# Five buffer counts and lead times of a planned schedule, and one sum moved from VectorE to a transfer, in a one-core attention trunk

## The chip, the core and the metric

One NeuronCore of one Trainium2 chip runs the whole program. TensorE (PE) multiplies matrices, VectorE (DVE) and ScalarE (ACT) work element by element, GpSimd (POOL) and SyncE (SP) here do little but issue transfers (DMA). The metric is device time in microseconds (us). The kernel before took 1747.45, 1742.09 and 1746.84 us in three runs, median 1746.84.

## The reference

The input is a residual stream of 256 tokens by 4096 channels, all in float32. Depth is one, so one layer runs, the attention layer:

```python
proj = rms_norm(x, norm_attn) @ w_in_attn        # 256x4096 @ 4096x16384 -> q | k | v | gate
o = stick_breaking_attention(q, k, v)            # 32 heads of 128
h = x + (o * silu(gate)) @ w_out_attn            # 256x4096 @ 4096x4096
return rms_norm(h, final_norm)
```

In the attention each weight is `sigmoid(z_ts) * prod_{s<j<t} (1 - sigmoid(z_tj))` for `s < t`, computed in log space with a suffix sum. The two projections are nearly all of the work: 320 MiB of float32 weights are read once.

## The kernel before

**Units.** The input projection is cut into 16 units. A unit makes 256 columns of each of q, k, v and gate, which is two heads. The output projection is cut into 4 more units of 1024 columns. A unit runs over the 4096 rows of its weights in 8 steps of 512 rows. One step needs 2 MB of weights, loaded as four *raw quarter tiles* of 128x1024 float32 (512 KB each, two 256 KB transfers from SP's queue). `raw{q}_{t}{k}` is the quarter of step q (counted over the whole program, 8 per unit) with column half t and row half k.

**Parts and products.** A matmul of float32 precision is made of three fast ones in the type fp32r: the operands are split into a high and a low half, and high*high, high*low and low*high are added up in PSUM. So for each *part* (a 128x1024 slice of weights) ScalarE casts the raw tile to fp32r (`wh{n}`, the high half), VectorE subtracts that from the raw tile (`wl{n}`, the low half), and then PE runs two to four *products*, each of three 128x128 by 128x512 matmuls. The names say it: `acc<-wh,sh` multiplies high by high, `acc<-wl,sh` is the matmul that first needs the low half (sh, sl: the halves of the activations in the input projection; oh, ol in the output projection).

**Seven instead of eight multiplications.** Some steps use a 2x2 scheme with seven block products in place of eight (Strassen and Winograd). Such a *seven step* has 7 parts and 14 products, and needs sums of raw tiles first: one is made by an accumulating transfer while weights are loaded (called T3 in the code; `raw<-in_w_in_dram` from POOL's queue), the other three by VectorE (`raw<-raw,raw`), or, in steps 1 and 3 of the input projection, the last of the three by an accumulating transfer between two tiles in the core's own memory (T4; `raw<-raw` from POOL's queue). An *eight step* has 4 parts and 16 products and no sums; a *mixed step* does half of its rows each way (6 parts, 15 products, three half-size sums). A unit of the input projection after the first has steps 1, 3, 4, 6 seven, 0, 2, 5 mixed and 7 eight: 117 products. In the output projection 1, 3, 6 are seven, 0, 2, 5 mixed, 4 and 7 eight: 119 products. The first unit of each projection is plain: 128 products.

**Evictions.** The products of a unit are added up in seven PSUM banks (`acc{u}_1` to `acc{u}_7`). When a unit ends, `combine` (L805) takes the banks out with VectorE and ScalarE into `qk_sb` and `gv_sb` (in the output projection into `h`). A bank that the next unit writes again has to be out before PE may start in it. Each input unit's two heads are computed while the next unit's products run, with small matmuls between the products (`ten`, L399).

**The planner.** Nothing of the order on the engines is written by hand. While the program is built, the class `Plan` plays it as a queue of events with costs per instruction; each engine takes, among the work that is ready, that with the smallest *key* (a due time in PE's time), and the order so found is the order in the program. Buffers are counted in *rings* (L413): a raw tile is taken before its load and given back when the last reader is done, a place for a low half is taken before the subtraction and given back when PE has finished the part. The same counts are the numbers of real buffers. On the chip every engine then works through its list strictly in order, and waits on semaphores.

The constants that matter here: `RAW_BUFS` (L46) raw quarter tiles; `PAIRS` (L47) high halves; `LOWS` (L47) low halves; `KEPT` (L48), the number of the program's last parts whose products are put in order of the PSUM bank (banks 4 and 5 first, then 2, then 3; L357), so that the last banks fill one after the other; `T3_LEAD` (L57), the time that the planner adds to the planned landing of an accumulating transfer before it lets its readers start; `FOURTH_IN`, `FOURTH_OUT` (L58), the seven steps whose last sum goes by transfer; `TEN_WAIT` (L62), the time that the planner lets pass before it offers a head's matmuls to PE; `EVICT` (L71), by how much the key of a unit's evictions on VectorE lies before the start of the next unit:

```python
key = place_of[u + 1, 0] - EVICT                                  # combine
fourth = not mixed and parts[a]["s"] in (FOURTH_IN if parts[a]["u"] < OUT0 else FOURTH_OUT)
```

`last_h` (L1208) and `finish` (L1291) end the program: token half 1 of the last 1024 columns is complete with banks 4 and 5, its sum of squares gives `factor1`, and the eight 128x512 tiles of that half are scaled and written; half 0 follows with banks 2 and 3 and `factor0`.

Of the kernel before, what the change touches and what calls it, by code (L numbers as in the profile page):

```python
# [42 lines left out]

SEVEN_IN, MIX_IN = (1, 3, 4, 6), (0, 2, 5)
SEVEN_AFTER, MIX_AFTER = (1, 3, 6), (0, 2, 5)
RAW_BUFS = 8  # L46
PAIRS, LOWS = 6, 6  # L47
KEPT = 6  # L48
LAST_STEPS = (2, 6, 5, 1, 0, 3, 7, 4)
LATE_FROM, LATE_BEHIND = 4, 1  # L50

# [2 lines left out]
HEADS_LATER = 12  # L54
AHEAD, SUMS_AHEAD = 1.0, 3.0
PIPE = 1
T3_LEAD = 1500  # L57
FOURTH_IN, FOURTH_OUT = (1, 3), ()  # L58
FOURTH_AHEAD = 6.0
RAW_LEAD = 0  # L60
EARLY = 2.5
TEN_WAIT = 1200  # L62
QK_LEAD = 2000
CAST_AHEAD = 3.0
BLOCKS_LATER = 2
# [2 lines left out]
FORM_LEAD = 0  # L68
STATS = 2, 10
AWAY, PLACE_H = (0, 1, 2), (0, 1, 0, 1, 0, 2)  # L70
EVICT = 0  # L71


PLAIN = {"C11": 1, "C21": 4, "C12": 7, "C22": 6}
# [60 lines left out]
def tensor_ns(n):  # L135
    return 0.4167 * n + 13.4 if n > 128 else 109.0
# [137 lines left out]
def kernel(  # L274
# [76 lines left out]
    n_parts = len(parts)  # L351
    kept = range(n_parts - KEPT, n_parts)
    begun = len(PLAIN_PARTS) * NS
    order = [(n, k) for n in range(begun) for k in range(len(parts[n]["prods"]))]
    order.sort(key=lambda e: (parts[e[0]]["s"], parts[e[0]]["prods"][e[1]][2]))
    order += [(n, k) for n in range(begun, n_parts - KEPT) for k in range(len(parts[n]["prods"]))]
    for banks in ((4, 5), (2,), (3,)):  # L357
# [41 lines left out]
    def ten(emit, *n):  # L399
        return nc.work("tensor", 90 + sum(tensor_ns(m) for m in n), emit, nc.here - 1e4, wait=TEN_WAIT)  # L400

# [10 lines left out]
    for name, places in (  # L412
        ("raw", RAW_BUFS), ("w", PAIRS), ("low", LOWS), ("gh", 3), ("one", 1), ("two", 1),  # L413
        ("qkh", 1), ("qkl", 1), ("f", 1), ("att", 1), ("heads", 1),
# [12 lines left out]
    def load():  # L427
# [8 lines left out]
        for _, q, t, k in sorted(tiles):  # L436
            if 1 < q < NS:
                yield nc.until(("used", 0, max(HALF * q - LOAD_AHEAD, 0)))
            yield nc.take("raw")
            raw[q, t, k] = wp.tile([P, HG, HALF, CW], F32, tag="raw", name=f"raw{q}_{t}{k}", bufs=RAW_BUFS)  # L440
            if seven[q] and (t, k) == (1, 0):
# [54 lines left out]
    def sums(q):  # L496
# [16 lines left out]

        yield nc.until(("T3", q), lead=T3_LEAD)
        yield nc.until(("lows", a))
# [9 lines left out]
        def moved_third():  # L525
# [5 lines left out]
            )  # L531
            yield nc.until(("T4", q), lead=T3_LEAD)
            nc.tell(("sums", g[0]))
# [271 lines left out]
    def combine(u, one, two, what):  # L805

        bank = ev[u]
        key = place_of[u + 1, 0] - EVICT

# [309 lines left out]
    def fetch():  # L1119

        yield nc.until("loaded", ("h", NJ - 3, 1))
        for c in AWAY:
            yield nc.take("raw")
            both = wp.tile([P, HG, HALF, CW], F32, tag="raw", name=f"back{c}", bufs=RAW_BUFS)
            for t in range(NT):
# [318 lines left out]
```

## Time and profile before

| | |
|---|---|
| three runs | 1747.45, 1742.09, 1746.84 us |
| the profiled execution | 1742.72 us, span of the core 1741.0 us, mean granted TensorE clock 0.996 |
| busy in the span | PE 1713.9, VectorE 1630.2, ScalarE 1227.0, POOL 209.1 us |
| DMA | 434.84 MB, mean 250 GB/s |

In the profile a row of a group gives the line, engine and operation, then out<-in by the program's names without numbers, the count, busy time and mean; "idle before" is the time that the engine stood still just before such an instruction, and the arrow names what ended it. Nearly all instructions carry line L158, that of the helper which records them, so the tiles' names tell them apart. A row of a timeline gives the start, the length and, in square brackets, the idle time before. PEld is the weight-load side of PE. A matmul's row lasts 0.39 us because neighbours overlap; the pitch from start to start is what counts.

### The profile page before, as it was taken

What the parts mean: (1) busy time and instruction counts of PE and PEld (TensorE: products, weight loads), DVE (VectorE), ACT (ScalarE), POOL (GpSimd) and SP (SyncE); (2) the same over time, 40 slices, a digit from 0 to 9 for tenths busy, and PEclk for the clock granted to TensorE, in tenths of its full rate; (3) what the DMA queues carried; (4) which work ended last, traced back from release to release, by engine and by line L of the source; (5) the groups of instructions that cost most, each with busy time, mean ns of one, the idle gap of its engine ahead of it and who ended that gap; (6) DMA issues with size and microseconds to landing.
All of it is one profiled execution on the core that took longest, in us unless ns stands there. A gap on an engine that the chain in (4) does not pass through costs nothing.

```text
span 1741.0 us, 23954 instructions
## 1 busy us (share of the span) xinstructions
PE 1713.9 (98%) x7690; PEld 1407.4 (81%) x7690; DVE 1630.2 (94%) x1872; ACT 1227.0 (70%) x1599; POOL 209.1 (12%) x224
## 2 busy tenths in 40 slices
PE   9999999999999999999999999999999999999997
PEld 6888888888888888888787878787888778888885
DVE  7889999999999999999999999999999987899997
ACT  7876777676777676767686767676767665666664
POOL 0010111011101011111111111111111022011100
PEclk9999999999999999999999999999999999999998
DMA  9998989888989898988888988889898778798886
GB/s 302 316 251 242 254 243 241 239 252 254 243 253 248 249 239 254 238 252 236 250 242 246 237 250 232 247 235 260 232 258 236 254 251 241 232 290 243 261 255 230
DMA packets 240543, 434.84 MB, mean 250 GB/s; under 512 B 25472, under 2 KB 45440, under 8 KB 240416
## 3 DMA queue, kind: packets, MB, share of 16 engines
q1 hardware_dynamic: 197616, 354.24, 62.0%
q0 software_dynamic: 41504, 77.22, 24.4%
q10 hardware_dynamic: 1296, 1.85, 0.3%
q8 instruction: 60, 0.98, 0.2%
q14 instruction: 67, 0.55, 0.1%
HBM read 407.52 MB, written 9.96 MB: 240 GB/s over the span
## 4 chain that ended last, share of the span: by engine, by line
PE 65%; DVE 13%; DMA 11%; issue 5%; ACT 4%; SPq 1%; POOL 0%; ACTq 0%; DVEq 0%; POOLq 0%
PE acc L158 62%; DMA raw<-in_w_in_dram 8%; DVE wl L158 8%; ACT wh L158 3%; DVE raw L158 3%; PE z L158 2%; DMA xres<-in_x_dram 1%; PE o L158 1%; SPq L158 1%; DMA p<-spill 1%; PE tr L158 1%; DMA raw<-in_w_out_dram 1%; ACT f L158 0%; DVE qk_sb L158 0%; DVE h L158 0%
## 5 line engine op out<-in xcount | busy, mean ns | idle before, releaser
L158 ACT CAST wh<-raw 128x1024 fp32r<-128x1024 f32 (+1 forms) x959 | 941.9, 1021 | 393.1 <-DMA raw<-in_w_in_dram 201.2
L158 DVE TENSOR_TENSOR wl<-raw,wh 128x1024 fp32r<-128x1024 f32 (+1 forms) x959 | 1100.8, 1184 | 60.3 <-ACT wh L158 57.0
L158 PE MATMUL acc<-wh,sh 128*128 128x512 f32 x1883 | 751.6, 399 | 4.3 <-DVE qk_sb L158 2.5
L158 PE MATMUL acc<-wl,sh 128*128 128x512 f32 x1883 | 735.9, 391 | 6.7 <-DVE wl L158 6.0
L158 PE MATMUL acc<-wh,sl 128*128 128x512 f32 x1883 | 735.6, 391 | 0.0
L158 PEld LDWEIGHTS acc<-wl,sh 128*128 128x128 f32 x1883 | 354.5, 188 | 85.2 <-DVE wl L158 15.7
L158 PEld LDWEIGHTS acc<-wh,sh 128*128 128x128 f32 x1883 | 354.2, 188 | 77.0 <-DVE qk_sb L158 5.8
L158 PEld LDWEIGHTS acc<-wh,sl 128*128 128x128 f32 x1883 | 353.8, 188 | 75.5 <-DVE sl L158 0.2
L158 DVE TENSOR_TENSOR raw<-raw,raw 128x1024 f32<-128x1024 f32 (+1 forms) x339 | 326.2, 964 | 2.0
L158 POOL DMA_DIRECT2D raw<-in_w_in_dram x105 | 127.9, 1218 | 931.6 <-DMA raw<-in_w_in_dram 522.9
L158 PE MATMUL acc<-wl,oh 128*128 128x512 f32 x485 | 189.5, 391 | 2.2 <-DVE wl L158 2.1
L158 PE MATMUL acc<-wh,oh 128*128 128x512 f32 x485 | 189.9, 391 | 0.0
L158 PE MATMUL acc<-wh,ol 128*128 128x512 f32 x485 | 188.8, 389 | 0.0
L158 PEld LDWEIGHTS acc<-wl,oh 128*128 128x128 f32 x485 | 91.1, 188 | 23.2 <-DVE wl L158 4.8
L158 PEld LDWEIGHTS acc<-wh,ol 128*128 128x128 f32 x485 | 91.1, 188 | 18.8
L158 PEld LDWEIGHTS acc<-wh,oh 128*128 128x128 f32 x485 | 91.1, 188 | 18.7
L158 ACT ACTIVATE f<-f 128x384 f32<-128x384 f32 x96 | 50.5, 526 | 3.0
L158 POOL DMA_DIRECT2D raw<-raw x30 | 26.5, 882 | 208.9 <-ACT f L158 86.7
L158 ACT CAST oh<-p 128x512 fp32r<-128x512 f32 (+3 forms) x41 | 19.3, 488 | 32.5 <-DVE p L158 16.6
L158 POOL DMA_DIRECT2D raw<-in_w_out_dram x18 | 21.5, 1192 | 136.2 <-DMA raw<-in_w_out_dram 105.4
L158 DVE SCALAR_TENSOR_TENSOR gv_sb<-acc,rin_v,gv_sb 128x512 f32<-128x512 f32 x45 | 33.5, 745 | 0.7
L158 POOL DMA_DIRECT2D p<-spill x41 | 22.9, 567 | 90.4 <-DVE ol L158 84.7
(88 smaller groups left out, 749.3 us busy)
## 6 DMA issues: line engine op xcount, KB each, us to landing
raw<-in_w_in_dram SPq DMA_DIRECT2D x1016, 256.0 KB, 5.0
raw<-in_w_out_dram SPq DMA_DIRECT2D x256, 256.0 KB, 5.1
raw<-in_w_in_dram POOLq DMA_DIRECT2D x60, 512.0 KB, 8.7
raw<-raw POOLq DMA_DIRECT2D x30, 512.0 KB, 6.8
raw<-in_w_in_dram POOLq DMA_DIRECT2D x45, 256.0 KB, 6.3
p<-spill POOLq DMA_DIRECT2D x41, 128.0 KB, 4.7
raw<-in_w_out_dram POOLq DMA_DIRECT2D x9, 512.0 KB, 8.8
xr<-in_x_dram SPq DMA_DIRECT2D x16, 256.0 KB, 5.5
```

Of the source, the lines that this page charges most:

```text
L158: return self.tc.keep_in_program_order(getattr(self.engine, name)(*args, **kw))
```

## The change

Six constants are different. The core gets nine raw quarter tiles (before: eight) and five places for low halves (six); both kinds take 4 KB per partition, so the sum is the same. Five parts (six) are ordered by bank at the end. The planner reckons with 2000 ns (1500) after an accumulating transfer, and with 1000 ns (1200) before a head's matmuls. In the output projection the last sum of step 1 goes by an accumulating transfer. The key of VectorE's evictions lies 3000 ns earlier.

```diff
-RAW_BUFS = 8
-PAIRS, LOWS = 6, 6
-KEPT = 6
+RAW_BUFS = 9
+PAIRS, LOWS = 6, 5
+KEPT = 5
...
-T3_LEAD = 1500
-FOURTH_IN, FOURTH_OUT = (1, 3), ()
+T3_LEAD = 2000
+FOURTH_IN, FOURTH_OUT = (1, 3), (1,)
...
-TEN_WAIT = 1200
+TEN_WAIT = 1000
...
-EVICT = 0
+EVICT = 3000
```

Through the planner the order on every engine shifts, though PE's products keep theirs up to the last unit's kept parts, and SP's loads of raw tiles keep theirs nearly everywhere. VectorE has three sums fewer (`raw137_01`, `raw145_01`, `raw155_01`, one in each mixed output unit), POOL three accumulating transfers more. At the end of the program SP issues the last weights (`raw159_11`) ahead of the last residual tiles (`grow`, `xres`) instead of behind them. Three places show what moves.

ScalarE at the end of unit 12 (the steps with raw tiles 100 to 103; the casts of parts 616 to 628), before:

```order
L158 CAST wh617_10112<-raw101_11_10078 128x1024
L158 CAST wh618_10122<-raw101_10_9892 128x1024
L158 CAST wh616_10099<-raw100_01_9929 128x1024
L158 CAST wh620_10164<-raw102_00_10125 128x1024
L158 CAST wh619_10142<-raw101_00_10001 128x1024
L158 CAST wh621_10181<-raw102_01_10136 128x1024
```

and now:

```order
L158 CAST wh617_10117<-raw101_11_10057 128x1024
L158 CAST wh616_10108<-raw100_01_9893 128x1024
L158 CAST wh618_10130<-raw101_10_9881 128x1024
L158 CAST wh619_10152<-raw101_00_9988 128x1024
L158 CAST wh620_10169<-raw102_00_10078 128x1024
L158 CAST wh621_10183<-raw102_01_10120 128x1024
```

The cast of part 619, whose raw tile is a sum made on the spot, stood behind the cast of the freshly loaded `raw102_00`, and now stands ahead of it.

VectorE over the border from unit 12 to unit 13 (the evictions `gv_sb12`, `qk_sb12` among the low halves of unit 13's first step), before:

```order
L158 TENSOR_TENSOR wl632_10334<-raw104_00_10282,wh632_10325 128x1024
L158 TENSOR_TENSOR gv_sb12_10245<-acc12_6_9734,gv_sb12_10245 128x512
L158 TENSOR_TENSOR wl633_10362<-raw104_01_10311,wh633_10356 128x1024
L158 TENSOR_TENSOR gv_sb12_10245<-acc12_7_9729,gv_sb12_10245 128x512
L158 SCALAR_TENSOR_TENSOR qk_sb12_10244<-acc12_2_9636,rin_v_1023,qk_sb12_10244 128x512
L158 TENSOR_TENSOR wl634_10378<-raw104_11_10322,wh634_10367 128x1024
L158 TENSOR_TENSOR raw104_00_10282<-raw104_00_10282,raw104_10_10196 128x2x256
L158 TENSOR_TENSOR wl635_10384<-raw104_10_10196,wh635_10376 128x1024
L158 SCALAR_TENSOR_TENSOR qk_sb12_10244<-acc12_4_9643,rin_v_1023,qk_sb12_10244 128x512
```

and now:

```order
L158 TENSOR_TENSOR gv_sb12_10249<-acc12_6_9738,gv_sb12_10249 128x512
L158 TENSOR_TENSOR wl632_10339<-raw104_00_10258,wh632_10325 128x1024
L158 TENSOR_TENSOR gv_sb12_10249<-acc12_7_9733,gv_sb12_10249 128x512
L158 TENSOR_TENSOR wl633_10363<-raw104_01_10292,wh633_10343 128x1024
L158 TENSOR_TENSOR raw104_00_10258<-raw104_00_10258,raw104_10_10176 128x2x256
L158 SCALAR_TENSOR_TENSOR qk_sb12_10248<-acc12_2_9651,rin_v_1026,qk_sb12_10248 128x512
L158 TENSOR_TENSOR wl634_10385<-raw104_11_10305,wh634_10362 128x1024
L158 SCALAR_TENSOR_TENSOR qk_sb12_10248<-acc12_4_9661,rin_v_1026,qk_sb12_10248 128x512
```

The eviction of bank 4 moved ahead of one low half (`wl635`), the one of bank 6 ahead of `wl632`.

VectorE at the end of the program, around the last bank, `acc19_3` (`back`, `h`: finished output tiles; `factor1` scales those of token half 1), before:

```order
L158 TENSOR_SCALAR back0_15691<-back0_15691,factor1_15818 128x512
L158 TENSOR_SCALAR back2_15709<-back2_15709,factor1_15818 128x512
L158 TENSOR_SCALAR h3_1_14247<-h3_1_14247,factor1_15818 128x512
L158 TENSOR_TENSOR h7_0_15681<-acc19_3_15177,h7_0_15681 128x256
L158 TENSOR_SCALAR h5_1_14966<-h5_1_14966,factor1_15818 128x512
L158 TENSOR_SCALAR h6_1_15664<-h6_1_15664,factor1_15818 128x512
L158 TENSOR_TENSOR h7_0_15681<-acc19_3_15177,h7_0_15681 128x256
L158 SCALAR_TENSOR_TENSOR most0_15872<-ssq_h_13651,mean_h0_15840 128x1
```

and now:

```order
L158 TENSOR_TENSOR h7_0_15719<-acc19_3_15179,h7_0_15719 128x256
L158 TENSOR_SCALAR back0_15671<-back0_15671,factor1_15824 128x512
L158 TENSOR_SCALAR back2_15705<-back2_15705,factor1_15824 128x512
L158 TENSOR_TENSOR h7_0_15719<-acc19_3_15179,h7_0_15719 128x256
L158 TENSOR_SCALAR h3_1_14246<-h3_1_14246,factor1_15824 128x512
L158 TENSOR_SCALAR h5_1_14967<-h5_1_14967,factor1_15824 128x512
L158 TENSOR_SCALAR h6_1_15694<-h6_1_15694,factor1_15824 128x512
L158 SCALAR_TENSOR_TENSOR most0_15871<-ssq_h_13648,mean_h0_15846 128x1
```

All five scalings of half 1 now stand behind the first addition that reads the last bank.

## The prediction

> **What bounds the kernel now.** I read the page's busy times and chain first.
>
> ```profile
> PE 1713.9 (98%) x7690; PEld 1407.4 (81%) x7690; DVE 1630.2 (94%) x1872; ACT 1227.0 (70%) x1599; POOL 209.1 (12%) x224
> PE 65%; DVE 13%; DMA 11%; issue 5%; ACT 4%; SPq 1%; POOL 0%; ACTq 0%; DVEq 0%; POOLq 0%
> ```
>
> PE sets the time, with VectorE close behind. How much PE loses is read from the windows view, cut at the first matmul of each unit (length first, then PE, PEld, DVE, ACT, POOL busy, clock, DMA share, GB/s).
>
> ```profile
> 7.09:97.73 90.64, 89.76 (x385) 73.14 (x386) 76.99 (x143) 76.96 (x147) 2.52 (x2) 0.98 0.96 319
> 440.73:525.69 84.96, 84.96 (x389) 70.56 (x388) 81.75 (x88) 61.95 (x77) 10.65 (x10) 1.00 0.89 247
> 610.77:695.73 84.96, 84.96 (x388) 70.57 (x387) 81.81 (x88) 62.11 (x77) 10.81 (x11) 1.00 0.87 247
> 1040.24:1128.00 87.76, 86.14 (x389) 70.26 (x387) 83.39 (x90) 61.32 (x78) 9.93 (x11) 1.00 0.87 239
> 1300.36:1388.17 87.81, 85.91 (x388) 70.28 (x387) 83.71 (x95) 63.67 (x80) 10.41 (x13) 1.00 0.85 249
> 97.73:1388.17 1290.44, 1282.09 (x5806) 1056.15 (x5805) 1237.79 (x1324) 929.93 (x1161) 161.17 (x154) 1.00 0.88 245
> 1482.36:1563.94 81.58, 81.23 (x358) 66.94 (x357) 75.59 (x77) 51.38 (x60) 9.54 (x10) 1.00 0.87 261
> 1563.94:1645.85 81.91, 81.29 (x358) 66.87 (x357) 77.80 (x82) 51.29 (x58) 8.28 (x8) 1.00 0.87 264
> 1645.85:1729.05 83.20, 82.01 (x358) 66.53 (x356) 77.45 (x94) 50.72 (x66) 3.56 (x3) 1.00 0.74 226
> ```
>
> The first row is the plain unit. The next two are units in which PE never stands still: 84.96 us is the floor of an input unit. Fifteen such units would take 1274.4 us; the sixth row shows 1290.4, so **16.0 us** are lost there. In the worst units (fourth and fifth row) length minus VectorE's busy time is 4.4 and 4.1 us, in the stall-free ones 3.2: where VectorE idles more, PE ends later. It has only some 2 us to spare per unit. The last three rows are the mixed output units.
>
> ```profile
> 1108.65 0.39 PE L158 MATMUL acc<-wl,sh 128*128 128x512 f32 x1
> ...
> 1111.14 0.39 PE L158 MATMUL acc<-wh,sh 128*128 128x512 f32 x1
> 1111.80 0.50 PE L158 MATMUL acc<-wl,sh 128*128 128x512 f32 x1 [0.27 <-DVE wl L158]
> ```
>
> From the first row to the second are 11 pitches, so the pitch is 0.2265 us; the third starts 0.43 us late, behind a low half. An output unit's 357 matmuls need 80.9 us at this pitch; three are 242.6 against 246.7 measured: **4.1 us** lost.
>
> Now the waits inside the fifteen input units (who waited for whom: total us, times, longest).
>
> ```profile
> SPq L158 <- DVE wl L158: 568.5, 305, 6.6
> ACT wh L158 <- DMA raw<-in_w_in_dram: 198.0, 130, 4.7
> DVE wl L158 <- ACT wh L158: 41.8, 58, 1.8
> PEld acc L158 <- DVE wl L158: 13.7, 20, 1.1
> PEld acc L158 <- DVE qk_sb L158: 5.8, 9, 1.1
> ```
>
> Read from above this is a loop: SP holds a load until VectorE gives a raw tile back, ScalarE waits for the load, VectorE for ScalarE's cast, PE's weight loads for VectorE's low half. The last row is the other kind of stall, a PSUM bank not yet evicted. The weight loads' waits overlap running matmuls, so I split the 16.0 us in their proportion: 11.2 us behind low halves, 4.8 us behind evictions.
>
> **The ninth raw tile.** One instance, in ScalarE's and VectorE's timelines:
>
> ```profile
> 1099.93 2.95 ACT L158 CAST wh<-raw 128x1024 fp32r<-128x1024 f32 x3 [3.96 <-DMA raw<-in_w_in_dram]
> 1101.96 2.37 DVE L158 TENSOR_TENSOR wl<-raw,wh 128x1024 fp32r<-128x1024 f32 x2 [1.26 <-ACT wh L158]
> ```
>
> ScalarE stood 3.96 us before the cast of `raw102_00`; the cast of part 619 behind it was ready, so VectorE lost 1.26 us just ahead of the stalls at 1111 us. I followed all 58 VectorE waits back along ScalarE. In 43, from
>
> ```profile
> 160.34 1.23 DVE L158 TENSOR_TENSOR wl<-raw,wh 128x1024 fp32r<-128x1024 f32 x1 [0.21 <-ACT wh L158]
> ```
>
> to
>
> ```profile
> 1364.95 1.83 DVE L158 TENSOR_TENSOR wl<-raw,wh 128x1024 fp32r<-128x1024 f32 x2 [0.81 <-ACT wh L158]
> ```
>
> they end at a raw tile that landed late: 33.1 us together, 79% of the 41.8. With one buffer more each load may go at about the time at which the load before it went. The gap between the two issues was 0.95 to 6.9 us in these 43 cases, and it covers the VectorE wait in nearly all. Beside that, 11 of them (like part 619) had their cast queued behind a load, and the new order puts it ahead. So 79% of the cause goes; I take off a tenth of it because loads in flight together land later, and count **-7.8 us** (70% of 11.2). Bounds: 0 if loads land no earlier, -11.2 if all stalls go.
>
> Here a rule on the transfers' ceiling bears on which bound is nearer. The Trainium skill, "DMA: Bandwidth & Descriptors", section "Specifications", states 358 GB/s from HBM for a core and 435 GB/s for its SBUF side; at the 247 GB/s above about a third would be free, and the term would be the full -11.2 us. The profile's share of 0.87 to 0.89 leaves only a tenth free, while the plain unit's 319 GB/s shows more; the tenth taken off stands for this doubt.
>
> **Five places for lows.** The price would be VectorE standing behind a low half whose place PE still holds. The trace shows the starts of all 955 low halves; I held each against PE's end of the part five before. Fifty would have had to wait, from
>
> ```profile
> 35.91 2.36 DVE L158 TENSOR_TENSOR wl<-raw,wh 128x1024 fp32r<-128x1024 f32 x2
> ...
> 1717.75 1.23 DVE L158 TENSOR_TENSOR wl<-raw,wh 128x1024 fp32r<-128x1024 f32 x1 [0.83 <-ACT wh L158]
> ```
>
> on; 18 lie in the fifteen units, none waiting 1 us, each with 4 us or more until PE needs it. (The first row's second low half is the first of the fifty.) Cost 0 in the sum, and a rival below. (The last is a kept part; the one five before it is kept no longer.)
>
> **Evictions first.** Bank 4 goes out ahead of a low half that takes
>
> ```profile
> 1126.69 1.22 DVE L158 TENSOR_TENSOR wl<-raw,wh 128x1024 fp32r<-128x1024 f32 x1
> 1127.83 0.74 DVE L158 SCALAR_TENSOR_TENSOR qk_sb<-acc,rin_v,qk_sb 128x512 f32<-128x512 f32 x1
> ```
>
> 1.14 us from start to start, more than the longest of the nine waits (1.1). The low half it passes ended at 1127.9, and PE's first matmul with it is
>
> ```profile
> 1135.60 0.39 PE L158 MATMUL acc<-wl,sh 128*128 128x512 f32 x1
> ```
>
> 7.7 us later, so its delay of 0.74 us hides. **-4.0 us** of the 4.8; bounds 0 and -4.8.
>
> **One sum by transfer.** VectorE loses three sums, POOL gets three transfers:
>
> ```profile
> L158 DVE TENSOR_TENSOR raw<-raw,raw 128x1024 f32<-128x1024 f32 x177 | 215.8, 1219 | 1.0
> L158 POOL DMA_DIRECT2D raw<-raw x30 | 26.5, 882 | 208.9 <-ACT f L158 86.7 <-DMA raw<-in_w_in_dram 81.5 <-DVE wl L158 10.3
> ```
>
> That frees 3.4 us of VectorE (1.14 each) in units where PE loses 4.1; POOL idles anyway, and behind its wait for the low half stands only the next step's T3, which has a step's time. The ninth tile helps here too. I take half, **-2.0 us**; bounds 0 and -4.1.
>
> **The end.** Five kept parts leave ten products behind banks 4 and 5 instead of twelve (counted in PE's order), so `factor1` comes 6 pitches, 1.36 us, later against PE's end. VectorE's last chain now:
>
> ```profile
> 1729.25 0.42 DVE L158 TENSOR_TENSOR h<-acc,h 128x256 f32<-128x256 f32 x1 [1.58 <-PE acc L158]
> 1729.59 0.87 DVE L158 TENSOR_SCALAR h<-h,factor 128x512 f32<-128x512 f32 x2
> 1730.38 0.42 DVE L158 TENSOR_TENSOR h<-acc,h 128x256 f32<-128x256 f32 x1
> 1730.71 0.15 DVE L158 SCALAR_TENSOR_TENSOR most<-ssq_h,mean_h 128x1 f32<-128x1 f32 x1
> 1731.43 0.16 DVE L158 SCALAR_TENSOR_TENSOR mean<-ssq_h,most 128x1 f32<-128x1 f32 x1 [0.57 <-ACT sq L158]
> ```
>
> Two scalings (0.79 us) stay between the additions; three more now come before `most`, at 0.40 each 1.2 us, of which 0.57 was idle: +0.6. All outputs of half 1 leave up to 1.36 us later. I take **+1.0 us**; bounds +0.6 and +1.4.
>
> T3_LEAD and TEN_WAIT only move places in the order; the waits they can touch are small on PE. 0, bounds ±1.
>
> A rule that would promise far more: the Trainium skill, "Trace Analysis", section "Identifying the Most-Contended Engine", judges nearness to the limit by weight-load occupancy, not matmul occupancy; 81% would leave 19%, over 300 us. The stall-free units stand at 70.56 of 84.96, or 83%, with PE never idle, so here the measure does not leave that room, and the sum goes by the floor.
>
> **The sum** against the profiled execution: 1742.7 - 7.8 - 4.0 - 2.0 + 1.0 = 1729.9 us. That execution and the three runs lie at 1742.1, 1742.7, 1746.8 and 1747.5, middle 1744.8, 2.1 above it; the median shown is 1746.84. For a run I forecast **1732 us**.
>
> **Rivals.** *Transfers bound.* If the DMA share of 0.89 is the real limit, more loads in flight land later by as much as they start earlier: terms one and three vanish, 1744.8 - 4.0 + 1.0 = 1742 us. For it: the share; against it: the plain unit moved 319 GB/s, and the worst units moved less (239) than the stall-free ones (247). *New waits for old.* The planner's costs are not the chip's; another order can stall elsewhere as much, 1744 us. For it: VectorE's 94%; against: no instruction was added to VectorE. *Slower: five places.* With loads early, VectorE runs further ahead, meets the cap at each unit border, and stands at its queue's head on PE's part of two products, 6 pitches or 1.36 us, with evictions behind it that PE needs next: 18 borders cost 24.5 us, and the eviction gain is gone: 1744.8 - 7.8 - 2.0 + 1.0 + 24.5 = 1760 us. It decides once the lead at the border exceeds about 7.7 us, which was just reached above; against it, most of the lead is made after the evictions.
>
> **How the numbers follow.** The forecast gets 0.65, transfers bound 0.13, new waits 0.11, five places 0.11. A change under 0.3% (5.2 us) cannot be told from none. Faster than 1741.6: the forecast and half of the border case 1742, 0.71; same 0.18; slower 0.11. The range runs from all stalls gone, 1742.7 - 16.0 - 4.1 + 0.6 = 1723, to the cases without gain with the upper run's level, 1747; the forecast's own is 1724 to 1739.
>
> **What would show it.** In the changed profile ScalarE's wait for raw tiles (198.0) at least halves, VectorE's for casts (41.8) falls under 20, PE's weight loads wait under 6 us for low halves and under 2 for evictions, and the fifteen units take about 1279 us. The end from PE's last matmul to the span's is longer by 0.6 to 1.4. If the waits for raw tiles stay while loads are issued earlier, transfers bound; if VectorE waits for PE before a low half, the places do.

## The result and the profile after

The changed kernel takes **1727.99 us** (median of four runs, 1726.04 to 1728.13), the kernel before took 1747.14 beside it (four runs, 1742.09 to 1750.38). The ratio is 0.9892, with a 95% interval of 0.9866 to 0.9919: faster, by 1.1%. Forecast were 1732 us in a range of 1723 to 1747. The profiled execution took 1728.01 us with a span of 1726.0.

The busy times and the engines' shares of the chain, as shown of before:

```profile
PE 1704.5 (99%) x7690; PEld 1410.3 (82%) x7690; DVE 1630.9 (94%) x1869; ACT 1243.6 (72%) x1599; POOL 211.9 (12%) x227
PE 96%; DVE 2%; DMA 1%; issue 1%; ACT 0%; SPq 0%; POOL 0%; ACTq 0%; DVEq 0%
```

The busy times hardly differ: VectorE has the same 94%. What changed is the chain: PE held 65% of it and now holds 96%, VectorE 13% and now 2%, transfers 11% and now 1%. The windows view, cut at the first matmul of each unit: the plain unit, the fifteen input units, one of these, then units 16 to 19:

```profile
7.78:99.12 91.34, 89.99 (x384) 73.02 (x385) 76.70 (x142) 76.97 (x147) 3.61 (x3) 0.98 0.96 324
99.12:1374.73 1275.61, 1274.58 (x5810) 1058.83 (x5809) 1242.50 (x1329) 947.44 (x1164) 160.12 (x154) 1.00 0.89 249
1035.03:1119.96 84.93, 84.93 (x391) 70.58 (x389) 82.75 (x89) 62.98 (x78) 10.68 (x10) 1.00 0.88 248
1374.73:1468.22 93.49, 92.38 (x420) 76.39 (x419) 76.45 (x133) 59.38 (x93) 22.95 (x39) 1.00 0.76 235
1468.22:1549.14 80.92, 80.92 (x359) 67.03 (x358) 75.14 (x77) 51.62 (x60) 10.39 (x11) 1.00 0.91 269
1549.14:1630.06 80.92, 80.92 (x359) 67.03 (x358) 76.52 (x80) 51.20 (x58) 9.22 (x9) 1.00 0.88 269
1630.06:1712.65 82.59, 81.38 (x358) 66.68 (x356) 76.22 (x91) 49.36 (x65) 4.46 (x4) 1.00 0.74 228
```

The fifteen input units take 1275.6 us (before 1290.4); units 2 to 15 take 84.92 or 84.93 us each with PE never idle, and only the first of the fifteen has a stall. Two of the three mixed output units stand at their floor of 80.9. The balance of the spans, 1741.0 to 1726.0: input units -14.8, mixed output units -2.3 (246.7 to 244.4), unit 16 -0.7, plain unit +0.7, the start before it +0.7, the end after PE's last matmul +1.4 (11.95 to 13.35), together -15.0.

Who waited for whom in the fifteen input units:

```profile
SPq L158 <- DVE wl L158: 507.2, 328, 6.0
ACT wh L158 <- PE acc L158: 203.8, 321, 2.9
ACT wh L158 <- DMA raw<-in_w_in_dram: 48.0, 37, 2.7
DVE wl L158 <- ACT wh L158: 2.3, 4, 0.7
PE acc L158 <- DVE wl L158: 1.0, 1, 1.0
PEld acc L158 <- DVE wl L158: 1.5, 1, 1.5
```

The loop has turned round. ScalarE waited 198.0 us for loads and now waits 48.0; VectorE waited 41.8 us for ScalarE's casts and now 2.3; no wait for an evicted bank is left. What ScalarE waits for now, 203.8 us in 321 pieces, is PE: a place for a high half that PE has not given back. The engines ahead of PE stand ready, and PE sets the pace.

The median landing of a 256 KB weight load, from the page's list of DMA issues, before

```profile
raw<-in_w_in_dram SPq DMA_DIRECT2D x1016, 256.0 KB, 5.0
```

and after:

```profile
raw<-in_w_in_dram SPq DMA_DIRECT2D x1016, 256.0 KB, 5.3
```

The count, the size and the time from issue to landing. Loads now land 0.3 us later after their issue, and still ScalarE waits a quarter as long for them.

The end, in VectorE's timeline:

```profile
1712.85 0.42 DVE L158 TENSOR_TENSOR h<-acc,h 128x256 f32<-128x256 f32 x1 [1.42 <-PE acc L158]
1713.19 0.87 DVE L158 TENSOR_SCALAR back<-back,factor 128x512 f32<-128x512 f32 x2
1713.98 0.42 DVE L158 TENSOR_TENSOR h<-acc,h 128x256 f32<-128x256 f32 x1
1714.31 1.27 DVE L158 TENSOR_SCALAR h<-h,factor 128x512 f32<-128x512 f32 x3
1715.50 0.15 DVE L158 SCALAR_TENSOR_TENSOR most<-ssq_h,mean_h 128x1 f32<-128x1 f32 x1
1715.75 0.16 DVE L158 SCALAR_TENSOR_TENSOR mean<-ssq_h,most 128x1 f32<-128x1 f32 x1
```

The three scalings behind the second addition hold up `most`; `mean` stands 2.90 us behind the first addition, 2.18 before. That is 0.7 of the 1.4 us by which the end is longer. The rest comes when the last output tiles leave; SP's issues of the last three of half 0, before

```profile
1734.15 2.78 SPq L158 DMA_DIRECT2D out_dram<-h  x3
```

and after:

```profile
1718.64 3.64 SPq L158 DMA_DIRECT2D out_dram<-h  x3
```

### The profile page after: what moved, and what is told of

Same layout as the page of the kernel before. It is cut to its first block, busy times and chain, and to the rows that moved or that the text cites. A ratio compares the mean times of both kernels' runs of the same rounds, so it can differ in the third digit from the quotient of the medians.

```text
span 1726.0 us, 24688 instructions
## 1 busy us (share of the span) xinstructions
PE 1704.5 (99%) x7690; PEld 1410.3 (82%) x7690; DVE 1630.9 (94%) x1869; ACT 1243.6 (72%) x1599; POOL 211.9 (12%) x227
## 3 DMA queue, kind: packets, MB, share of 16 engines
q10 hardware_dynamic: 1296, 1.85, 0.3%
## 4 chain that ended last, share of the span: by engine, by line
PE 96%; DVE 2%; DMA 1%; issue 1%; ACT 0%; SPq 0%; POOL 0%; ACTq 0%; DVEq 0%
PE acc L158 91%; PE z L158 2%; PE o L158 2%; PE tr L158 1%; DVE wl L158 1%; DMA p<-spill 1%; DMA raw<-in_w_out_dram 0%; DMA raw<-in_w_in_dram 0%; DVE raw L158 0%; DVE h L158 0%; DVE ol L158 0%; DVE p L158 0%; ACT wh L158 0%; ACT oh L158 0%; ACT f L158 0%
## 5 line engine op out<-in xcount | busy, mean ns | idle before, releaser
L158 ACT CAST wh<-raw 128x1024 fp32r<-128x1024 f32 (+1 forms) x959 | 961.5, 1023 | 387.8 <-PE acc L158 262.6
L158 DVE TENSOR_TENSOR raw<-raw,raw 128x1024 f32<-128x1024 f32 (+1 forms) x336 | 322.3, 964 | 2.8
L158 POOL DMA_DIRECT2D raw<-raw x33 | 31.0, 938 | 155.6 <-DVE wl L158 137.0
```

What stands on the lines that cost most here:

```text
L158: return self.tc.keep_in_program_order(getattr(self.engine, name)(*args, **kw))
```

## The experiments

The theory after the result: the ninth raw tile alone takes the lateness out of the input units, and with it both kinds of stalls, since VectorE is no longer late for anything; the rest of the change matters only at the end. The rivals: each part carries its own term, as the prediction had it; or the new order does it, and the tile is only something that the planner counts.

### The tile and the order

Two runs on the kernel before, planned anew:

```diff
-PAIRS, LOWS = 6, 6
-KEPT = 6
+PAIRS, LOWS = 6, 5
+KEPT = 5
```

and in the first of them also

```diff
-RAW_BUFS = 8
+RAW_BUFS = 9
```

> The kernel before with nine raw tiles, five places for lows and five kept parts; eviction keys, sums, T3_LEAD and TEN_WAIT as before. Theory (raw supply): most of the loss in the fifteen input units goes, they take 1274.4 + about 6 us, and the run is 1731 to 1736 us; PE's weight loads still wait 3 to 6 us for evictions (qk_sb). Rival (the other constants do it): 1741 to 1748 us. Rival (transfers bound): ScalarE's wait for raw tiles stays near 198 us and the time near 1742.

> The kernel before with five places for lows and five kept parts, still eight raw tiles. Theory: five places cost nothing in the units, the end is 0.6 to 1.4 us longer: 1742 to 1749 us, the ratio to before within 0.3% of 1. Rival (five places make VectorE stand at its queue's head): 10 us or more slower, with VectorE waiting for PE before low halves.

The third parts the planner's count from the real buffers, so that the order is held still: it has the second's constants and its order on all engines, and one real tile more where the raw tiles are allocated:

```diff
-bufs=RAW_BUFS
+bufs=RAW_BUFS + 1
```

The fourth is the changed kernel with eight raw tiles:

```diff
-RAW_BUFS = 9
+RAW_BUFS = 8
```

> The order of the run with eight raw tiles and five places, instruction by instruction, but nine real raw tiles under it: the planner still counts eight. Theory (raw supply): loads go earlier although the order is the old one; 32 of the 43 late casts need no other order, so the run gains at least half of what nine planned tiles gain: 1733 to 1740 us. Rival (the planner's order does it): no gain, 1742 to 1749 us, since casts still stand behind loads in ScalarE's list.

> The changed kernel with eight raw tiles again, all other five changes kept (five lows, five kept parts, eviction keys, one more sum by transfer, T3_LEAD, TEN_WAIT). Theory (raw supply): the waits behind low halves come back, minus the eviction gain of about 4 us and the output units' 2 us: 1737 to 1743 us. Rival (the other constants do it): 1727 to 1731 us.

Measured beside one kernel before (1745.99 us, 15 runs from 1742.67 to 1751.69):

| | median (range), us | ratio, interval | fifteen input units |
|---|---|---|---|
| nine tiles, five places, rest as before | 1734.66 (1731.23 to 1739.37) | 0.9924, 0.9894 to 0.9954 | 1275.0 |
| eight tiles, five places, rest as before | 1736.98 (1732.91 to 1740.67) | 0.9938, 0.9916 to 0.9961 | 1282.4 |
| the same order, nine real tiles | 1726.89 (1724.62 to 1727.44) | 0.9875, 0.9846 to 0.9905 | 1274.8 |
| the changed kernel, eight tiles | 1749.22 (1741.34 to 1754.55) | 1.001, 0.9992 to 1.0027 | 1295.8 |

The first came within its theory's time, but without the waits for evictions that the theory still expected; the second and third came faster than both of their forecasts, the fourth slower than both.

The pair that differs in nothing but the real tile is the second and third. The input units of the second (columns as in the prediction):

```profile
98.11:1380.47 1282.36, 1278.48 (x5806) 1057.17 (x5805) 1235.41 (x1324) 936.48 (x1161) 161.29 (x154) 1.00 0.89 247
```

and the waits in them:

```profile
ACT wh L158 <- DMA raw<-in_w_in_dram: 162.6, 116, 4.5
PEld acc L158 <- DVE wl L158: 5.6, 11, 1.1
PEld acc L158 <- DVE qk_sb L158: 3.5, 3, 1.6
```

The input units of the third:

```profile
99.03:1373.80 1274.77, 1274.77 (x5806) 1058.37 (x5805) 1235.04 (x1324) 945.03 (x1162) 161.11 (x154) 1.00 0.90 249
```

and the waits in them, of which PE has none:

```profile
ACT wh L158 <- DMA raw<-in_w_in_dram: 62.1, 59, 3.3
DVE wl L158 <- ACT wh L158: 18.9, 29, 0.9
```

With the tile, PE is busy for all of the 1274.77 us, and neither kind of stall is left, **although the eviction key is 0 in both**. VectorE still waits 18.9 us for casts there, and PE does not see it. The planner need not even know of the tile. In the changed kernel the tile, together with the order that is planned for it, is worth 1749.2 - 1728.0 = 21 us, and without them the rest of the change brings nothing (ratio 1.001). A second pair holds this order still as well: the last run below has the order of the fourth on every engine and nine real tiles. It takes 1731.07 us instead of 1749.22 (ratios to the kernel before 0.9883 and 1.001), and its input units 1275.0 instead of 1295.8. So the order-only rival falls: the same tile brings 10 us in one order and 18 in the other. The first run has stall-free input units too, and loses in the output projection: units 16 to 19 take 96.5, 85.8, 84.9 and 84.4 us there (below).

The second run's gain of 9 us, with eight tiles, was the surprise. Is it the cap on the chip or the order that the planner found with it? The second run's constants and order with six real places, where the low halves are allocated:

```diff
-bufs=LOWS
+bufs=LOWS + 1
```

> Exactly the order of the run with only five places for lows (eight raw tiles), but the core holds six places. It tells whether that run's unexpected gain of 9 us came from the order that the planner found, or from the places themselves (VectorE held back at a cap). Theory, the order: the input units take 1282 us again, 1735 to 1739 us. Rival, the cap on the chip: without it the input units go back to 1290 us, 1745 us.

1735.12 us (ten runs, 1734.32 to 1741.13), ratio 0.9932, 0.9907 to 0.9958: the gain stays without the cap, so it is the order's. (The profiled execution was the second highest of the ten, and its input units took 1287.1 us; the medians carry this.) With eight tiles the input units take 1282 us in the second run's profile (1287 in this one's, of the same order), 1290 in the order of before and 1296 in that planned from the changed constants: how the stalls fall is open to the order. Whether five places are held or six makes no difference that the runs can tell (1736.98 and 1735.12, the ranges overlap). With nine real tiles they take 1275 to 1279 in every order that was run.

### The eviction key

The changed kernel without the key:

```diff
-EVICT = 3000
+EVICT = 0
```

> The changed kernel with the eviction key back at 0. Theory: with nine tiles VectorE is early enough that no eviction holds PE whatever the key; input units stay at 1275 to 1276 us with under 0.5 us of PE waits behind qk_sb; 1727 to 1729 us. Rival (the key was worth 4.0 us, as predicted): 1732 us, with PE waits behind qk_sb of about 5 us.

The kernel before with the key:

```diff
-EVICT = 0
+EVICT = 3000
```

> The kernel before with the eviction key at 3000 and nothing else. Theory: with eight tiles the input units go on losing to late loads, and the new order only deals the stalls out anew: input units 1282 to 1296 us, ScalarE's wait for raw tiles 160 to 200 us; 1737 to 1750 us. Rival (the predicted -4.0 us for this part): input units 1286 us, PE's waits behind qk_sb under 2 us, 1742 us, and the waits behind low halves as before (about 14 us).

Without the key the changed kernel takes 1727.92 us (1725.88 to 1728.67), input units 1275.4: no difference, and PE waits for no eviction in them. With the key and eight tiles, 1746.42 us (1743.04 to 1749.87), ratio 1.0006, 0.9982 to 1.0029: no gain. The input units of the latter:

```profile
97.81:1390.56 1292.75, 1283.56 (x5811) 1055.90 (x5809) 1238.03 (x1324) 927.73 (x1163) 160.85 (x154) 1.00 0.88 245
```

and the weight loads' waits in them:

```profile
PEld acc L158 <- DVE wl L158: 20.3, 31, 1.1
PEld acc L158 <- DVE gv_sb L158: 0.5, 1, 0.5
```

The key did what it says: the nine waits behind `qk_sb` are gone. But the waits behind low halves rose from 13.7 to 20.3 us, and the input units take 1292.8 instead of 1290.4. A VectorE that is late for the sum of its work only chooses with such a key what it is late for.

### The sum by transfer

The changed kernel without it:

```diff
-FOURTH_IN, FOURTH_OUT = (1, 3), (1,)
+FOURTH_IN, FOURTH_OUT = (1, 3), ()
```

> The changed kernel with the fourth sum of the output units back on VectorE (FOURTH_OUT empty), all else as changed. Theory: with the planner counting on nine tiles the residual tiles come late in the output units, as in the run with only nine tiles and five places (units 16 to 19: 96.5, 85.8, 84.9, 84.4 us there), and the transfer sum cures that: input units stay at 1275 to 1276 us, the four output units take 348 to 352 us instead of 337.9, the end is 12.0 us instead of 13.4; 1735 to 1741 us. Rival (my prediction's price, VectorE's 3.4 us and half of that on PE): output units 340 us, 1729 us.

The kernel planned for eight and holding nine raw tiles (the third run above) with it:

```diff
-FOURTH_IN, FOURTH_OUT = (1, 3), ()
+FOURTH_IN, FOURTH_OUT = (1, 3), (1,)
```

> As the run that plans with eight raw tiles and holds nine, with the transfer sum in the output units added. Theory: those units hardly stall there (93.8, 80.9, 80.9, 83.3 us), so VectorE's three sums less bring 0 to 2.3 us, and the order at the end costs 0 to 1.4 us: 1725 to 1728 us. Rival (fewer sums on VectorE speed the output units by themselves): 1722 us or less.

Without the transfers the changed kernel takes 1733.55 us (nine runs, 1731.3 to 1737.41), 5.6 more. Its four output units take 344.8 us instead of 337.9: between the two forecasts, under the theory's 348 and well over the rival's 340. The three mixed ones:

```profile
1467.07:1551.77 84.70, 82.88 (x359) 67.99 (x358) 76.26 (x78) 51.51 (x60) 9.56 (x10) 0.98 0.83 251
1551.77:1634.28 82.51, 81.22 (x359) 66.93 (x357) 77.34 (x81) 50.70 (x58) 8.29 (x8) 1.00 0.87 259
1634.28:1718.88 84.60, 82.01 (x358) 66.53 (x356) 78.24 (x95) 50.24 (x66) 3.57 (x4) 1.00 0.71 215
```

and the waits in them on which the reading rests (the groups of VectorE and of PE):

```profile
DVE h L158 <- DMA xres<-in_x_dram: 6.4, 6, 2.3
PE acc L158 <- DVE wl L158: 5.7, 5, 1.8
```

VectorE stands 6.4 us at additions of residual tiles (`xres`) that have not landed, with low halves behind them in its queue, and PE 5.7 us for low halves. With the transfers the same waits are 1.9 and 1.2 us. (Unit 17 loses nearly 1.8 us more to a slower clock behind one of these stalls; see the last section.) That the three sums themselves were too much for VectorE is not the reason: in the order planned for eight tiles, with nine held, all three sums on VectorE, units 17 and 18 stand at 80.92 already. There the transfers bring 1725.41 us (1724.33 to 1726.52) against 1726.89, which the runs cannot part. So in the changed kernel the transfer pays by what comes with it, the place at which VectorE reaches the residual tiles. SP does not issue them earlier: counted in the two traces, the eight of units 17 and 18 go out after as many weight loads as without the transfers, or after two to four more. But VectorE has one to four more low halves ahead of each of their additions. This is read from the two orders; neither was changed by itself.

This pair also settles the end: without the transfers the span ends 11.9 us after PE's last matmul, as before, with five kept parts; the runs with five kept parts and `FOURTH_OUT` empty, five of them, all end 11.9 to 12.0 us after it. With the key or the two lead times undone it stays at 13.3. The transfers alone do not make it so either: the three runs that have them and are planned for eight tiles end 12.3, 12.3 and 12.8 us after it. The longer end takes the transfers and the count of nine together.

### The lead times, fewer places, and the planner's count

All three start from the changed kernel. The lead times of before:

```diff
-T3_LEAD = 2000
-TEN_WAIT = 1000
+T3_LEAD = 1500
+TEN_WAIT = 1200
```

> The changed kernel with the planner's two lead times back at 1500 and 1200 ns. Theory: they only move places in an order whose input units have slack; 1727 to 1729 us, input units 1275 to 1276 us. Rival: they carry part of the gain, 1731 us or more.

1728.37 us (1726.88 to 1729.31), input units 1275.0: worth nothing, as the prediction took them.

Four places for lows:

```diff
-PAIRS, LOWS = 6, 5
-KEPT = 5
+PAIRS, LOWS = 6, 4
+KEPT = 4
```

> The changed kernel with four places for lows instead of five (and four kept parts, which the planner needs then). It doses the rival 'slower: five places', by which VectorE stands at its queue's head until PE is done with a part, with evictions behind it. Theory: VectorE's waits for PE before a low half grow from about 0.4 us in an input unit to some us, all of it slack, and PE stays stall-free; input units 1275 to 1277 us, 1726 to 1731 us. Rival: one wait of 1.36 us or more at each unit border that PE sees, 1740 to 1755 us.

1733.35 us (seven runs, 1731.14 to 1736.94): some 5 slower than five places, and between the two forecasts. The rival's picture is not what happened: the input units take 1278.7 us, and VectorE waited for PE before a low half in them only twice:

```profile
DVE wl L158 <- PE acc L158: 2.1, 2, 1.3
```

PE's longest wait in unit 16:

```profile
PE o L158 <- ACT gated L158: 2.4, 1, 2.4
```

No stall at every border, then. The dearest unit is 16 with 96.0 us (93.5 in the changed kernel); its longest stall stands before a head's matmul that waited for ScalarE (the changed kernel has the same one, 1.1 us). This kernel is slower, but not by the queue that the rival named. Its order is a new one and it keeps four parts, so what the place itself costs is left open.

The planner's count set to eight, while the core holds nine raw tiles:

```diff
-RAW_BUFS = 9
+RAW_BUFS = 8
...
-bufs=RAW_BUFS
+bufs=RAW_BUFS + 1
```

> The changed kernel with the planner counting eight raw tiles while the core holds nine. Theory: as in the run that did this to the order of before with the transfer sum (1725.4 us), the ninth tile works without the planner's knowledge, and the residual tiles come in time: input units 1275 us, output units 337 us, the end 12.3 us; 1724 to 1727 us. Rival: the planner has to know of the tile for the last microseconds, 1728 us or more.

1731.07 us (four runs, 1726.38 to 1731.52), where the theory had 1724 to 1727. The input units came as it said (1274.96), but unit 16 took 96.9 us and unit 19 85.0, with a stall of 2.2 us and a slower clock behind it (last section). This is the other half of the second pair above: the order is that of the changed kernel with eight tiles, instruction by instruction, and the tile alone takes it from 1749.22 to 1731.07. By the number it is the rival's case; but the kernel of 1725.4 us does without the planner's knowledge of the tile, so what I had wrong was to carry the good output units of a neighbouring order over to this one.

The lowest median is that of the kernel before planned for eight raw tiles, five places and five kept parts, with nine tiles held and the transfer sum: **1725.41 us**, ratio 0.9875 (0.9832 to 0.9917) to the kernel before; without the transfer sum it takes 1726.89, and the two ranges overlap. In the same comparison the changed kernel without its key, which is as fast as the changed kernel, took 1727.92; the ranges 1724.33 to 1726.52 and 1725.88 to 1728.67 still touch.

## Why the prediction was right, and where its steps were not

**The floor** held: fifteen times 84.96 us, 1274.4, is where the input units now stand but for 1.2 us; the first of them stands 1.7 above it, the others 0.03 below.

**The ninth tile** was sized at -7.8 us of a possible 11.2. The mechanism was right, and the size too small, on two counts. The tenth taken off for later landings was not needed: landings grew from 5.0 to 5.3 us, and no stall came of it. And the term ended at the stalls behind low halves. In the first pair that differs in the tile alone, both kinds of stalls went, and the input units took 7.6 us less; in the second pair, 20.8 us less. The tile takes away what the order loses, down to the floor. The order of before was not run with nine tiles; that the whole -14.8 us of its input units is the tile's is concluded from the other orders, which all come to 1275 to 1279 us with it and none without it. The Trainium skill's ceilings ("DMA: Bandwidth & Descriptors", "Specifications"), weighed in the prediction, had spoken for the full term, and the trace agrees with that reading: at a DMA share of 0.89 and 249 GB/s the transfers still had the room to come earlier.

**Evictions first**, -4.0 us, is the step that failed. The place was right and the cause wrong. I had treated the split of 16.0 us into 11.2 and 4.8 as two faults with two cures. They were one fault, a late VectorE, seen at two places. The key alone moves its stalls from one place to the other (1746.42 us); with the tile, the key has nothing to do (1727.92 without it). The term is worth 0.

**Five places**: cost 0, as forecast. What they are for is the room: a ninth tile takes the 4 KB per partition that the sixth place had. Nine tiles with six places were not run. The waits that the prediction counted do occur where VectorE now runs ahead, in the changed kernel's mixed output units:

```profile
DVE wl L158 <- PE acc L158: 8.0, 8, 1.5
```

The longest is of the size of the rival's 1.36 us, and of the three units, which all hold such waits, two stand at the floor: nothing that PE needed next was late behind them.

**One sum by transfer**, -2.0 us: the three mixed units fell by 2.3, but not for the reason given. I priced the instructions that VectorE loses. What counted was where VectorE reaches the residual tiles: in this order 5.6 us in the median hang on it, in another nothing that can be measured. That the number fits is luck.

**The end**, +1.0 us between +0.6 and +1.4, came to +1.4. The chain was read rightly, five scalings behind the first addition, and `mean` comes 0.7 us later for it, where +0.6 was worked out. Its origin was read wrongly: I blamed the five kept parts, and with these alone the end is as before. The order there came with the transfer sums and the count of nine. The other 0.7 us, in the issue of the last output tiles, was not traced further.

**The rivals.** Transfers as the bound predicted that loads issued earlier land later by as much; they landed 0.3 us later. New waits for old is what the eight-tile version of the change does (1749.22 us); nine tiles leave room for a poor order. The slow case did not come, for the reason given under the five places.

**The sum** against the profiled execution was -12.8 us and came to -14.7 (-15.0 between the spans): input units -14.8 where -11.8 stood, mixed output units -2.3 for -2.0, the end +1.4 for +1.0, and +0.7 in the start, the plain unit and unit 16 together, which had no term. That it came so near is in part luck: of the 11.8 us, 4.0 were booked under the key and brought by the tile. The signposts all came: ScalarE's wait for loads more than halved, VectorE's for casts fell under 20, and PE's waits under their marks; the fifteen units took 3 us less than the 1279 named.

## What to carry to other kernels

When a chain of engines feeds the one that sets the pace, stalls at its different inputs may be one lateness; trace them to the first engine that waits for something outside, and don't add up a cure for each. To price a buffer, hold the order still and add the real buffer alone: an order planned anew with another count can move the time by as much as the buffer does. A loop that has one buffer to spare also forgives a poor order and late transfers, and this shows as units that are alike to a few hundredths of a microsecond.

## What the runs showed of the hardware that was not expected

**A stall of two microseconds can cost nearly two more.** In the run without transfer sums, PE's timeline from the longest stall of unit 17:

```profile
1507.89 0.39 PE L158 MATMUL acc<-wh,oh 128*128 128x512 f32 x1
1510.10 0.50 PE L158 MATMUL acc<-wl,oh 128*128 128x512 f32 x1 [1.82 <-DVE wl L158]
...
1512.10 0.63 PE L158 MATMUL acc<-wh,ol 128*128 128x512 f32 x1
...
1514.66 0.51 PE L158 MATMUL acc<-wh,ol 128*128 128x512 f32 x1
1515.00 0.39 PE L158 MATMUL acc<-wh,oh 128*128 128x512 f32 x1
```

PE idled 1.82 us; about 1.4 us after it started again, its matmuls went at a pitch of 0.427 us (six in 2.56 us) instead of 0.2265, for some 3.4 us. The unit lost 2.0 us to the stall and nearly 1.8 to the clock; its row above has PE busy 82.88 us for work of 80.92. The run with only nine tiles and five places shows it in three of its output units (granted clock 0.98 there), which is part of why its profiled execution took 1739.37 us, the slowest of its four.

It does not follow every such stall: one of 2.4 us in the run with four places and one of 1.8 us in the changed kernel with eight tiles were followed by full speed. What decides can be read from the traces. The granted clock changes on a fixed beat of 3.41 us: in the run with only nine tiles and five places the three slow stretches begin at 1416.73, 1515.72 and 1601.05 us, 29 and 25 beats of 3.413 us apart, and each lasts one beat. The windows view cut at these beats (length, then PE's busy time; the clock is the third from the end), for the stall above:

```profile
1508.07:1511.48 3.41, 1.59 (x7) 1.16 (x7) 3.27 (x4) 2.18 (x4) 1.16 (x1) 1.00 0.85 315
1511.48:1514.89 3.41, 3.41 (x10) 2.63 (x9) 3.41 (x4) 1.57 (x2) 0.61 (x1) 0.50 0.88 222
```

for the changed kernel with eight tiles:

```profile
1708.78:1712.20 3.42, 1.66 (x8) 1.30 (x8) 3.42 (x4) 3.31 (x6) 0.00 (x0) 1.00 0.27 85
1712.20:1715.61 3.41, 3.41 (x17) 2.80 (x16) 3.41 (x4) 2.78 (x3) 0.00 (x0) 1.00 0.99 294
```

and for the run with four places:

```profile
1414.62:1418.04 3.42, 1.89 (x9) 1.23 (x7) 2.90 (x6) 1.58 (x4) 0.54 (x1) 1.00 1.01 379
1418.04:1421.45 3.41, 2.50 (x12) 2.14 (x13) 2.65 (x6) 2.32 (x4) 0.00 (x0) 1.00 0.64 202
```

The stall of 2.4 us lies across a border between two beats, and PE is busy for 1.89 us of the first and 2.50 of the second. From the first input unit on to PE's last matmul, the 14 profiles of this case have five beats in which PE was busy for less than 1.6 us (1.59 in the stall above; 1.53, 1.25 and 1.20 in the run with only nine tiles and five places; 1.21 in unit 19 of the changed kernel planned for eight tiles and holding nine), and each is followed by one at half clock. After every other beat, all with more than 1.64 us, the clock stayed full. So a stall's price depends on how much of one beat it takes, and no run controlled where it falls. This is a reading of these profiles, not a test. The Trainium skill, "TensorE: Matmul & The Clock Gate", section "Part 1: The HAM clock gate (the 'warmup' mystery)", tells of a clock halved after an idle window of about 3.4 us, in windows that run freely. The halved pitch agrees with its 426.7 ns for 512 columns, and the beat with its free-running window; the idle time does not, since 1.8 us within one window sufficed here, and the measurement decides.

**Spread.** The kernel before ranged from 1737.02 to 1760.25 us over all comparisons, the changed one over 2.1 us in its four runs, and the fastest one over 2.2: I read this as transfers that vary from run to run and no longer reach PE; it was not tested by itself. Nine tiles alone do not give it: runs with nine tiles and stalls in the output units spread over 5 to 8 us.
